# Hybrid encoder block: weight-piece rings of five places instead of four, room taken from GpSimd's DMA scratch, and a head whose ScalarE queue issues two loads

## The chip, the cores and the metric

The kernel runs on one core of a Trainium2 chip. The metric is the device time of one launch in microseconds (us); lower is better. A profile is one execution recorded by the hardware profiler. The engines are named as the profile names them: PE is the matrix engine (PEld its weight loads), DVE is VectorE, ACT is ScalarE, POOL is GpSimd, SP is SyncE. ACTq, SPq and POOLq stand for the DMA issues of these engines. TensorE's granted clock is a fraction of full speed.

## The reference

One encoder layer on a batch of 512 tokens and another of 256, 768 tokens in all, in float32. Cut to what matters:

```python
h = rmsnorm(x, ln_mix_g)
z = h @ w_in                       # 2048 -> 2560: [fourier 1024 | q 1024 | k 256 | v 256]
of = fourier_mix(zf, w_fourier)    # Re(fft2) per channel group, then a 128x128 map
oa = window_attention(rope(q), rope(k), v, attn_sink)      # 16 heads, window +-128
mixed = concat([rmsnorm(of, g_f), rmsnorm(oa, g_a)])
x = x + mixed @ w_out              # 2048 -> 2048
h = rmsnorm(x, ln_mlp_g)
u = relu(h @ w_up)                 # 2048 -> 8192
x = x + (u * u) @ w_down           # 8192 -> 2048
y = rmsnorm(x, ln_final_g)
```

## The kernel before

**Arithmetic.** Every float32 operand of a product is split in two float32r parts: a high part, which ACT makes by a rounding copy, and a low part, which DVE makes by subtracting the high part from the source. A product is then three matmuls, high by high, high by low and low by high. So each piece of a weight matrix passes four stations: a DMA on SP's queue brings a raw piece of 512 KB into the pool `wpool` (tag `raw`, two places), ACT writes the high part (`wh`, four places), DVE writes the low part (`wl`, four places), and PE uses both. A place of `wh` or `wl` is free again when the last matmul that reads it is done. A place takes 4 KB of each of SBUF's 128 partitions.

**Stages, in the order of the program.**

- Head (0 to 44 us): the v projection. `load_k` brings 16 slices `xk` of x, transposed, `split_x` scales them by the norm's gains (`gains`, a small table) and splits them into `hh` and `hl`. `load_wv` brings v's columns of w_in in four tiles `wr` of four slices each, and `split_wv` splits them. The matmuls are in `v_step` (L222, product `pv`). The tokens' norms come from rows of x (`xt`, L215). The order of the instructions on ACT, DVE and SP is the order of the code here. ACT's queue issues `gains`, the first two `wr` tiles (the first in three parts) and `ident`, before ACT's first computation. SP's queue issues the slices of x.
- Projection of q, k and the fourier group (44 to 387 us): 36 pieces of w_in through `wsplit` (L82), 48 matmuls to a piece (L542, product `pz`), with the rotation of q and k and the fourier transforms beside it.
- Attention, and the fourier half of the output projection (387 to 603 us). w_out comes in 32 pieces of two k-slices by 512 columns, numbered i = 0 to 31. `out_load(i)` issues the load, `out_high(i)` (L163) makes the high part and `out_low(i)` (L174) the low part. Pieces 0 to 15 belong to the fourier half (four blocks n of 512 output columns, four pieces to a block), pieces 16 to 31 to the attention half. The matmuls are in `proj_step` (L739, product `pm`): 24 of them, eight k-steps of three, for one row block m of 128 tokens and one n. In this stage all engines run by a planned order: `job` states each piece of work with its engine, a cost, a due time and what it has to follow, and the list scheduler `in_turn` puts the jobs of all engines in one order (by the earliest possible start and then by the due time). The jobs ("hi", i) and ("lo", i) follow `last` (L801), the last matmul of the piece i-4, which leaves the place of the ring to the piece i. The job ("load", i) follows hi and lo of the piece i-2, which leaves its raw place.
- The attention half of the output projection (603 to 751 us): block by block, n = 0 to 3, each with three groups of two row blocks; a group has eight k-steps of six matmuls. GpSimd's queue adds the fourier half onto x (`yp<-y`, L944, two transfers to a group). Pieces 20 to 31 are split here, and ACT, DVE and SP are put in order by the framework's scheduler.
- The MLP up (751 to 1685 us, `pu` L1034) and down (1685 to 2599 us, `pd` L1315), in a Strassen-like scheme of fewer products. Weight pieces go through the same two rings: `up_high` (L1013), `up_low` (L1019) and the sums of pieces (L1290).
- The tail (to 2611 us): the last residual, the final norm, and the store.

PE's own order is the order of the code in all stages. POOL's DMAs are those whose descriptors are made in software; they take their room from a scratch area in SBUF, of 16,384 bytes of each partition unless the program states another figure (L1503).

Of the kernel before, what the change touches and what calls it, by code (L numbers as in the profile page):

```python
# [11 lines left out]
F32 = mybir.dt.float32  # L12
F32R = mybir.dt.float32r
# [27 lines left out]
def hybrid_encoder(ctx: ExitStack, tc: tile.TileContext, a: dict):  # L41
# [37 lines left out]

    def wsplit(raw, g=None):  # L80

        hi = wpool.tile(raw.shape, F32R, tag="wh", name="wh", bufs=4)  # L82
        lo = wpool.tile(raw.shape, F32R, tag="wl", name="wl", bufs=4)
        if g is None:
            split(hi[:], lo[:], raw[:])
        else:
            for i in range(raw.shape[1]):
                split(hi[:, i, :], lo[:, i, :], raw[:, i, :], g(i))
        return hi, lo
# [70 lines left out]
    def out_high(i):  # L160
        half, n, j = out_seq[i]
        raw = raws[i]
        wh = wpool.tile([P, 2, 512], F32R, tag="wh", name="wh", bufs=4)  # L163
        if half:
            for r in range(2):
                nc.scalar.activation(wh[:, r], raw[:, r], AF.Copy, scale=gcat[:, 8 + 2 * j + r : 9 + 2 * j + r])
        else:
            nc.scalar.activation(wh[:], raw[:], AF.Copy)
        out_w[half, n].append((wh, None))

    def out_low(i):
        half, n, j = out_seq[i]
        raw, wh = raws.pop(i), out_w[half, n][j][0]
        wl = wpool.tile([P, 2, 512], F32R, tag="wl", name="wl", bufs=4)  # L174
        if half:
            for r in range(2):
                nc.vector.scalar_tensor_tensor(  # L177
                    out=wl[:, r], in0=raw[:, r], scalar=gcat[:, 8 + 2 * j + r : 9 + 2 * j + r], in1=f32(wh[:, r]),
                    op0=ALU.mult, op1=ALU.subtract,
                )  # L180
        else:
            nc.vector.tensor_tensor(out=wl[:], in0=raw[:], in1=f32(wh[:]), op=ALU.subtract)  # L182
        out_w[half, n][j] = (wh, wl)
# [8 lines left out]
    with ExitStack() as ph:  # L192
# [9 lines left out]
        with tc.tile_pool(name="xp", bufs=2, reuse_waits="tile") as xp:  # L202

            def load_x(m):
                xt = xp.tile([P, D], F32, tag="xt", name=f"xt{m}", bufs=2)
                nc.sync.dma_start(xt[:], x_rows(m))
                return xt

            def load_k(k):
                xk[k] = xp.tile([P, T], F32, tag="xk", name="xk", bufs=7)  # L210
                for t in (slice(0, HALF), slice(HALF, T)) if k == 0 else (slice(0, T),):
                    nc.sync.dma_start(xk[k][:, t], a["x_t"][k * P : (k + 1) * P, t])

            def row_norm(m, xt):
                nc.scalar.activation(xt[:], xt[:], AF.Square, accum_out=ss0[:, m : m + 1])  # L215
                rsqrt_of(r0[:, m : m + 1], ss0[:, m : m + 1], D, 1, nc.gpsimd)

            def v_step(k, n, ms):
                j, i = k // 4, k % 4
                l, r = ((hh, 0), (hl, 0), (hh, 1))[n]  # L220
                for m in ms:
                    nc.tensor.matmul(  # L222
                        pv[m][:, :256], l[j][:, i, m * P : (m + 1) * P], wv[j][r][:, i, :],
                        start=(k == 0 and n == 0), stop=(k == NK - 1 and n == 2),
                    )

            def v_take(m):
                pg = pv[m][:, :256].rearrange("p (g d) -> p g d", g=NKV)
                split(vhl[:, m, :, 0, :], vhl[:, m, :, 1, :], pg, r0[:, m : m + 1])

            def row_scale(m):

                dg = zp.tile([P, T], F32, tag="zs", name="dg")[:, :P]
                nc.gpsimd.tensor_scalar(
                    out=dg, in0=ident[:], scalar1=r0[:, m : m + 1], scalar2=1.0, op0=ALU.mult, op1=ALU.mult
                )
                pb = pp.tile([P, 512], F32, tag="f", name="pb", bufs=2)
                nc.tensor.matmul(pb[:, :P], ones[:], dg, start=True, stop=True)
                nc.scalar.copy(rb[:, m * P : (m + 1) * P], pb[:, :P])

            def load_wv(j, queue):
                pool, tag = (xp, "wr") if j < 2 else (wpool, "raw")
                wr = pool.tile([P, 4, 256], F32, tag=tag, name="wr", bufs=2)
                for i in ((0, 1), (1, 2), (2, 4)) if j == 0 else ((0, 4),):
                    i = slice(*i)
                    queue.dma_start(wr[:, i], w_in[:, 4 * j : 4 * j + 4, IN_W - 256 :][:, i])
                raw_v[j] = wr
                wv[j] = [wpool.tile([P, 4, 256], F32R, tag=c, name=c, bufs=4) for c in ("wh", "wl")]

            def split_wv(j, i):  # L250
                i = slice(*i)
                split(wv[j][0][:, i], wv[j][1][:, i], raw_v[j][:, i])

            def split_x(k, t=slice(0, T)):
                j, i = k // 4, k % 4
                split(hh[j][:, i, t], hl[j][:, i, t], xk[k][:, t], gains[:, k : k + 1])

            xk, xts, raw_v, wv, done = {}, {}, {}, {}, []
            pv = [pp.tile([P, 512], F32, tag="ps", name="pv") for _ in range(NM)]
            hand = ("Activation", "DVE", "SP")  # L260
            with tc.manual_schedule(engines={getattr(mybir.EngineType, e) for e in hand}):
                nc.scalar.dma_start(gains[:], a["c_gains"])
                load_wv(0, nc.scalar)
                for k in range(7):
                    load_k(k)
                    if k == 1:
                        load_wv(1, nc.scalar)
                nc.scalar.dma_start(ident[:], a["c_ident"])
                split_x(0, slice(0, HALF))
                split_wv(0, (0, 1))  # L270
                split_x(0, slice(HALF, T))
                split_wv(0, (1, 2))
                for k in range(NK):
                    if k + 1 < NK:
                        split_x(k + 1)
                    if k == 0:
                        split_wv(0, (2, 4))
                    if k % 4 == 2 and k // 4 < 3:
                        split_wv(k // 4 + 1, (0, 4))
                    if k + 7 < NK:  # L280
                        load_k(k + 7)
                    if k in (0, 3):
                        load_wv(2 + k // 3, nc.sync)
                    if k in (8, 9):
                        xts[k - 8] = load_x(k - 8)
                    for n in range(3):
                        v_step(k, n, range(NM if k < 8 else 4))
                for m in range(4):
                    row_norm(m, xts[m])
                    if m + 2 < NM:  # L290
                        xts[m + 2] = load_x(m + 2)
                for k in range(8, NK):
                    for n in range(3):
                        v_step(k, n, (4, 5))
                for m in range(NM):
                    if m >= 4:
                        row_norm(m, xts[m])
                    v_take(m)
# [499 lines left out]
    for i in range(3, 22):  # L798
        half, n, j = out_seq[i]
        need = 6 * SLOT * (n + 4 * half) + 1.4 * j  # L800
        last = ("mm", out_seq[i - 4][1], NM - 1, 2 * out_seq[i - 4][2] + 1) if i >= 4 else None  # L801
        job(("load", i), SP, 1.5, need - 14, lambda i=i: out_load(i), ("hi", i - 2), ("lo", i - 2), start=-22, wait=5)
        if i < 20:
            job(("hi", i), ACT, 1.2 if half else 0.96, need - 5, lambda i=i: out_high(i), ("load", i), last, ("<", ("hi", i - 1)), start=8.3 * i - 24)
# [205 lines left out]

    def up_high(u, s):
        raw = uw[u, steps[s][0]]
        wh = wpool.tile([P, 4, 256], F32R, tag="wh", name="wh", bufs=4)  # L1013
        nc.scalar.activation(wh[:], raw[:], AF.Copy)  # L1014
        ux[u, s] = (raw, wh)

    def up_low(u, s):
        raw, wh = ux[u, s]
        wl = wpool.tile([P, 4, 256], F32R, tag="wl", name="wl", bufs=4)  # L1019
        nc.vector.tensor_tensor(out=wl[:], in0=raw[:], in1=f32(wh[:]), op=ALU.subtract)  # L1020
        ux[u, s] = (wh, wl)

# [258 lines left out]
    def sums(u):  # L1281
# [5 lines left out]
        for t, o in ws:  # L1287
            if o is not None:
                add(t, o, ALU.subtract if i in (2, 3) else ALU.add)
            wh = wpool.tile([P, 1024], F32R, tag="wh", name="wh", bufs=4)  # L1290
            wl = wpool.tile([P, 1024], F32R, tag="wl", name="wl", bufs=4)
            nc.scalar.activation(wh[:], t[:], AF.Copy)  # L1292
            whl.append((wh, wl, t))
        if len(ss) > 1:
# [195 lines left out]
def _layouts(given):  # L1490
# [2 lines left out]
    return {  # L1493
        "x_t": np.concatenate([given["x_prompt"], given["x_sample"]], 0).T,
        "c_gains": np.concatenate(gains).reshape(3 * NK, P).T,
    }


# [23 lines left out]
```

## Time and profile before

| | us |
|---|---|
| time, median of 3 runs | 2613.86 (2612.37 to 2613.91) |
| the profiled execution's own time | 2613.02 |
| its span in the trace | 2611.2 |
| PE busy | 2584.0 (99% of the span), 13556 matmuls |
| DVE busy | 1702.9 (65%) |
| ACT busy | 1048.1 (40%) |
| POOL busy | 245.2 (9%) |
| matmuls start | 7.79 |
| last matmul ends | 2599.5 |

The span runs from the first to the last instruction; the time of the profiled execution has 1.8 us around it. PE is occupied nearly all the time, so the page's shares alone do not say what an edit around PE may be worth; the waits of PE, the stretches in which it stood still, and the two ends without any matmul do. These lines are shown in the prediction. "Busy" of a matmul overlaps with the next one's, so the distance between the starts of two matmuls (0.173 us at 384 columns, 0.227 us at 512 columns in undisturbed stretches) is the better measure of PE's pace.

### The profile page before, as it was taken

Reading aid. Unit: us, or ns where it says so; the run is one execution under the profiler, and the core shown is the slowest. Engines: PE = TensorE matmul, PEld = TensorE weight load, DVE = VectorE, ACT = ScalarE, POOL = GpSimd, SP = SyncE. Lnnn points to the kernel's source line nnn. Section 1 sums busy time; section 2 is a strip of 40 time slices with the busy share of each in tenths; the row PEclk is TensorE's granted clock in tenths of the full one; section 3 lists DMA queues with packets and bytes.
Section 4 is the critical chain, followed back from the end, with each engine's and each line's share of the span. In section 5 each row is a group of like instructions: output and inputs, shape, how many; then the busy total and the mean of one; then the engine's idle time right before and its main releaser. Section 6 shows DMA issues by size and latency. Waiting matters only on the chain.

```text
span 2611.2 us, 34913 instructions
## 1 busy us (share of the span) xinstructions
PE 2584.0 (99%) x13556; PEld 2363.5 (91%) x13556; DVE 1702.9 (65%) x2085; ACT 1048.1 (40%) x1506; POOL 245.2 (9%) x357
## 2 busy tenths in 40 slices
PE   8999999999999999999999999999999999999998
PEld 8999998887899999999999999988888888888886
DVE  4344546775655665555877787767776765777677
ACT  6233316664333333333544454433333333333335
POOL 1011212332100011000000000010000000000000
PEclk9999999999999999999999999999999999999999
DMA  8333577557774545448666666685543662554364
GB/s 298 118 116 126 161 236 208 151 140 183 216 216 153 176 164 179 173 164 317 205 211 215 231 232 210 206 338 177 181 159 111 216 235 81 178 180 160 99 210 147
DMA packets 278982, 488.23 MB, mean 187 GB/s; under 512 B 21216, under 2 KB 171488, under 8 KB 277792
## 3 DMA queue, kind: packets, MB, share of 16 engines
q1 hardware_dynamic: 202240, 329.91, 39.5%
q10 hardware_dynamic: 54576, 96.58, 9.7%
q0 software_dynamic: 22000, 59.52, 8.2%
q8 instruction: 106, 1.74, 0.3%
q14 instruction: 60, 0.49, 0.1%
HBM read 359.30 MB, written 126.62 MB: 186 GB/s over the span
## 4 chain that ended last, share of the span: by engine, by line
PE 80%; DMA 3%; DVE 2%; ACT 1%; issue 1%; POOL 0%; SPq 0%; ACTq 0%; POOLq 0%; DVEq 0%
PE pu L1034 36%; PE pd L1315 34%; PE pm L739 7%; DMA raw<-in_w_out 1%; DMA qh<-rh 1%; PE s L584 1%; PE o L655 1%; PE t L638 1%; DMA ry<-zq 0%; DMA zq<-zs 0%; PE ptx L132 0%; DVE wl L182 0%; DMA oar<-oadl 0%; DVE wl L177 0%; DVE acc L1249 0%
## 5 line engine op out<-in xcount | busy, mean ns | idle before, releaser
L1034 PE MATMUL pu<-xf,wh 128*128 128x384 f32 x3328 | 848.7, 336 | 0.0
L1034 PEld LDWEIGHTS pu<-xf,wh 128*128 128x128 f32 x3328 | 600.5, 188 | 1.7 <-ACT o L1052 1.2
L1034 PE MATMUL pu<-xf,wl 128*128 128x384 f32 x1664 | 559.1, 336 | 0.0
L1315 PE MATMUL pd<-wh,sh 128*128 128x512 f32 x1320 | 513.5, 389 | 0.0
L1315 PE MATMUL pd<-wl,sh 128*128 128x512 f32 x1320 | 513.5, 389 | 0.0
L1315 PE MATMUL pd<-wh,sl 128*128 128x512 f32 x1320 | 513.5, 389 | 0.0
L1292 ACT ACTIVATE wh<-rd 128x1024 fp32r<-128x1024 f32 x200 | 202.2, 1054 | 524.1 <-PE pd L1315 425.1
L1302 DVE TENSOR_TENSOR wl<-rd,wh 128x1024 fp32r<-128x1024 f32 x200 | 236.1, 1221 | 229.3 <-ACT wh L1292 228.7
L1014 ACT ACTIVATE wh<-ur 128x1024 fp32r<-128x1024 f32 x160 | 169.9, 1062 | 374.1 <-PE pu L1034 209.1
L1034 PEld LDWEIGHTS pu<-xf,wl 128*128 128x128 f32 x1664 | 312.8, 188 | 0.0
L1315 PEld LDWEIGHTS pd<-wh,sl 128*128 128x128 f32 x1320 | 247.8, 188 | 51.5
L1315 PEld LDWEIGHTS pd<-wl,sh 128*128 128x128 f32 x1320 | 247.8, 188 | 51.3
L1315 PEld LDWEIGHTS pd<-wh,sh 128*128 128x128 f32 x1320 | 247.8, 188 | 51.3
L1020 DVE TENSOR_TENSOR wl<-ur,wh 128x1024 fp32r<-128x1024 f32 x160 | 195.5, 1222 | 81.5 <-ACT wh L1014 78.4
L1055 DVE TENSOR_TENSOR o<-pu,o 128x768 f32<-128x768 f32 x160 | 152.9, 956 | 118.2 <-PE pu L1034 114.4
L542 PE MATMUL pz<-hh,wh 128*128 128x384 f32 x576 | 147.4, 336 | 0.0
L542 PE MATMUL pz<-hh,wl 128*128 128x384 f32 x576 | 146.4, 334 | 0.9 <-DVE wl L68 0.9
L542 PE MATMUL pz<-hl,wh 128*128 128x384 f32 x576 | 146.2, 334 | 0.0
L1285 DVE TENSOR_TENSOR rd<-rd 128x1024 f32<-128x1024 f32 x112 | 131.7, 1217 | 0.0
L1014 ACT ACTIVATE wh<-sx 128x1024 fp32r<-128x1024 f32 x64 | 67.9, 1062 | 127.7 <-PE pu L1034 99.4
L542 PEld LDWEIGHTS pz<-hh,wl 128*128 128x128 f32 x576 | 104.0, 188 | 1.3 <-DVE wl L68 1.3
L1305 DVE TENSOR_TENSOR sl<-sr,sh 128x768 fp32r<-128x768 f32 x110 | 104.6, 951 | 0.0
(210 smaller groups left out, 3463.9 us busy)
## 6 DMA issues: line engine op xcount, KB each, us to landing
rd<-in_w_down SPq DMA_DIRECT2D x176, 512.0 KB, 5.3
ur<-in_w_up SPq DMA_DIRECT2D x128, 512.0 KB, 4.0
sr<-sd SPq DMA_DIRECT2D x94, 384.0 KB, 5.5
pd<-o ACTq DMA_DIRECT2D x64, 384.0 KB, 2.3
o<-pd POOLq DMA_DIRECT2D x64, 384.0 KB, 6.2
sd<-sm ACTq DMA_DIRECT2D x60, 384.0 KB, 2.6
raw<-in_w_in SPq DMA_DIRECT2D x36, 512.0 KB, 3.6
raw<-in_w_out SPq DMA_DIRECT2D x32, 512.0 KB, 5.5
```

What stands on the lines that cost most here:

```text
L542: nc.tensor.matmul(ps[c][s][:, :HALF], w[:, i, cs], h[j][:, i, s * HALF : (s + 1) * HALF], start=first and n == 0, stop=last and n == 2,)
L584: nc.tensor.matmul(st["s", h], st["qs"][:, h, :], kd[:, g, k0 * P : k0 * P + nk], start=(n == 0), stop=(n == 1))
L739: nc.tensor.matmul(ps[:], l(k), w[:, k % 2, :], start=(k == 0 and n == 0), stop=(k == 7 and n == 2))
L1014: nc.scalar.activation(wh[:], raw[:], AF.Copy)
L1020: nc.vector.tensor_tensor(out=wl[:], in0=raw[:], in1=f32(wh[:]), op=ALU.subtract)
L1034: nc.tensor.matmul(ps[:, t, :HALF], w[:, i, t * P : (t + 1) * P], xb[:, o, i, :], start=(s == first_of[bank] and i == 0 and n == 0), stop= ...
L1055: nc.vector.tensor_tensor(out=o, in0=src, in1=o, op=ALU.add)
L1285: add = lambda x, y, op: nc.vector.tensor_tensor(out=x[:], in0=x[:], in1=y[:], op=op)
L1292: nc.scalar.activation(wh[:], t[:], AF.Copy)
L1302: nc.vector.tensor_tensor(out=wl[:], in0=t[:], in1=f32(wh[:]), op=ALU.subtract)
L1305: nc.vector.tensor_tensor(out=sl[:], in0=sr[:], in1=f32(sh[:]), op=ALU.subtract)
L1315: nc.tensor.matmul(ps[m][:, ns], l[:, q, ts], w[:, ns], start=(j == 0 and q == 0 and t == 0), stop=(j == HP // 2 - 1 and q == 1 and t == 2),)
```

## The change

**Rings.** `wh` and `wl` get five places each instead of four, at every line where one of their tiles is made. That is 8 KB more of each partition, and `dynamic_dma_scratch_size=8192` takes these 8 KB from the scratch area of POOL's DMAs. In the planned stage `last` names the piece i-5 instead of i-4.

**Head.** ACT's queue issues two loads, `gains` and the first slice of the first `wr` tile. Then a small Square of six columns of the constant tile `mhalf` is put ahead of ACT's other work (its result, in `ss0`, is overwritten later). The other slices of the first `wr` tile, the second tile and `ident` are issued on SP's queue, between the slices of x. A new input `w_v` holds v's 256 columns of w_in, laid out on the host so that the slices of one partition lie side by side: a row of a `wr` part is one stretch of 1, 3 or 4 KB, where it was one stretch of 1 KB to a slice.

```diff
@@ wsplit, out_high, out_low, up_high, up_low, the sums of pieces
-        hi = wpool.tile(raw.shape, F32R, tag="wh", name="wh", bufs=4)
-        lo = wpool.tile(raw.shape, F32R, tag="wl", name="wl", bufs=4)
+        hi = wpool.tile(raw.shape, F32R, tag="wh", name="wh", bufs=5)
+        lo = wpool.tile(raw.shape, F32R, tag="wl", name="wl", bufs=5)
...
@@ load_wv
-            def load_wv(j, queue):
-                pool, tag = (xp, "wr") if j < 2 else (wpool, "raw")
-                wr = pool.tile([P, 4, 256], F32, tag=tag, name="wr", bufs=2)
-                for i in ((0, 1), (1, 2), (2, 4)) if j == 0 else ((0, 4),):
+            def load_wv(j, queue, parts=((0, 4),)):
+                if j not in raw_v:
+                    pool, tag = (xp, "wr") if j < 2 else (wpool, "raw")
+                    raw_v[j] = pool.tile([P, 4, 256], F32, tag=tag, name="wr", bufs=2)
+                    wv[j] = [wpool.tile([P, 4, 256], F32R, tag=c, name=c, bufs=5) for c in ("wh", "wl")]
+                wr = raw_v[j]
+                for i in parts:
                     i = slice(*i)
-                    queue.dma_start(wr[:, i], w_in[:, 4 * j : 4 * j + 4, IN_W - 256 :][:, i])
-                raw_v[j] = wr
-                wv[j] = [wpool.tile([P, 4, 256], F32R, tag=c, name=c, bufs=4) for c in ("wh", "wl")]
+                    queue.dma_start(wr[:, i], a["w_v"][:, 4 * j : 4 * j + 4][:, i])
@@ the head
                 nc.scalar.dma_start(gains[:], a["c_gains"])
-                load_wv(0, nc.scalar)
-                for k in range(7):
+                load_wv(0, nc.scalar, ((0, 1),))
+                nc.scalar.activation(ss0[:], mhalf[:, :NM], AF.Square)
+                load_k(0)
+                load_wv(0, nc.sync, ((1, 4),))
+                for k in range(1, 7):
                     load_k(k)
-                    if k == 1:
-                        load_wv(1, nc.scalar)
-                nc.scalar.dma_start(ident[:], a["c_ident"])
+                    if k == 2:
+                        load_wv(1, nc.sync)
+                nc.sync.dma_start(ident[:], a["c_ident"])
@@ the planned stage
-        last = ("mm", out_seq[i - 4][1], NM - 1, 2 * out_seq[i - 4][2] + 1) if i >= 4 else None
+        last = ("mm", out_seq[i - 5][1], NM - 1, 2 * out_seq[i - 5][2] + 1) if i >= 5 else None
@@ the host's layouts, and the program
+        "w_v": given["w_in"][:, IN_W - 256 :].reshape(NK, P, 256).transpose(1, 0, 2),
...
-    nc = bacc.Bacc("TRN2", target_bir_lowering=False, num_devices=1)
+    nc = bacc.Bacc("TRN2", target_bir_lowering=False, num_devices=1, dynamic_dma_scratch_size=8192)
```

Line numbers of the changed kernel are three or four higher from the head on. The change moves instructions at three places that matter below.

In the head, ACT's first instructions before (`wr` is v's weight tile; the numbers behind names tell tiles apart):

```order
L262 DMA gains_264<-in_c_gains 128x48
L246 DMA wr_307<-in_w_in 128x256 x2
L246 DMA wr_307<-in_w_in 128x2x256
L246 DMA wr_318<-in_w_in 128x4x256
L268 DMA ident_65<-in_c_ident 128x128
L70 ACT_TABLE_LOAD
L70 ACTIVATE hh0_286<-xk_313,gains_264 128x384
L67 ACTIVATE wh_311<-wr_307 128x256
```

and ACT's first instructions after the change:

```order
L263 DMA gains_264<-in_c_gains 128x48
L249 DMA wr_307<-in_w_v 128x256
L265 ACT_TABLE_LOAD
L265 ACTIVATE ss0_265<-mhalf_68 128x6
L70 ACTIVATE hh0_286<-xk_312,gains_264 128x384
L67 ACTIVATE wh_308<-wr_307 128x256
```

Four DMA issues have left ACT, and the load of its function table stands ahead of the first instruction that needs data from a DMA.

At the end of the projection of q, ACT's rows around the high part of the last piece of w_in (`wh_3830`) before; `rh` is the high part of a rotated q, `qh2` and `ql2` are where q's parts are stored:

```order
L70 ACTIVATE rh_3822<-rx_3812 128x384
L458 DMA qh2_88<-rh_3822 128x384
L459 DMA ql2_89<-rl_3823 128x384
L67 ACTIVATE wh_3830<-raw_3828 128x1024
L70 ACTIVATE rh_3906<-rx_3896 128x384
```

and after:

```order
L70 ACTIVATE rh_3664<-rx_3654 128x384
L462 DMA qh2_88<-rh_3664 128x384
L463 DMA ql2_89<-rl_3665 128x384
L67 ACTIVATE wh_3830<-raw_3828 128x1024
L70 ACTIVATE rh_3743<-rx_3733 128x384
L462 DMA qh2_88<-rh_3743 128x384
L463 DMA ql2_89<-rl_3744 128x384
L70 ACTIVATE rh_3822<-rx_3812 128x384
```

The high part of that piece has moved ahead of the splits of two queries (`rh_3743` and `rh_3822`).

At the boundary between the two halves of the output projection, ACT's rows before; the two rows with `gains` ahead of `xc` are the pieces 16 and 17, the two behind it 18 and 19 (a piece is two instructions); `xc` takes the last result of the fourier half, `oar` and `oah5` belong to the norm of the attention rows:

```order
L705 ACTIVATE oar_6304<-oar_6304 128x512
L166 ACTIVATE wh_6431<-raw_6058,gains_264 128x512 x2
L166 ACTIVATE wh_6439<-raw_6081,gains_264 128x512 x2
L752 ACTIVATE xc_6466<-pm_6415,r1_267 128x512
L166 ACTIVATE wh_6469<-raw_6459,gains_264 128x512 x2
L166 ACTIVATE wh_6475<-raw_6464,gains_264 128x512 x2
L696 ACTIVATE oah5_6478<-oar_6409 128x512
```

and after, where the first two are the pieces 17 and 18:

```order
L709 ACTIVATE oar_6312<-oar_6312 128x512
L166 ACTIVATE wh_6439<-raw_6076,gains_264 128x512 x2
L166 ACTIVATE wh_6447<-raw_6126,gains_264 128x512 x2
L756 ACTIVATE xc_6474<-pm_6423,r1_267 128x512
L166 ACTIVATE wh_6477<-raw_6467,gains_264 128x512 x2
L700 ACTIVATE oah5_6483<-oar_6417 128x512
L700 ACTIVATE oah5_6483<-oar_6419 128x512
L166 ACTIVATE wh_6764<-raw_6472,gains_264 128x512
```

The piece 16 has left this place. Its two instructions now stand five row blocks earlier on ACT, ahead of the `xc` of the last column block's first row block (`es` and `ob` belong to the attention):

```order
L618 ACTIVATE es_6057<-es_6057 128x4
L166 ACTIVATE wh_6083<-raw_5991,gains_264 128x512 x2
L666 COPY ob_6104<-o_6072 128x512
L756 ACTIVATE xc_6120<-pm_6019,r1_267 128x512
```

In the same way the first piece of each other column block behind the first (the pieces 4, 8 and 12) stands four or five row blocks earlier on ACT than before, and the load of the piece two behind it as much earlier on SP's queue. Of the four pieces of a block, ACT then has two at the place where it had the first two, now the second and the third, and one where it had the last two.

More of the change, by code (lines that the diff above doesn't have):

```diff
@@ L162, in out_high @@
         raw = raws[i]
-        wh = wpool.tile([P, 2, 512], F32R, tag="wh", name="wh", bufs=4)
+        wh = wpool.tile([P, 2, 512], F32R, tag="wh", name="wh", bufs=5)
         if half:
@@ L173, in out_low @@
         raw, wh = raws.pop(i), out_w[half, n][j][0]
-        wl = wpool.tile([P, 2, 512], F32R, tag="wl", name="wl", bufs=4)
+        wl = wpool.tile([P, 2, 512], F32R, tag="wl", name="wl", bufs=5)
         if half:
@@ L1012, in up_high @@
         raw = uw[u, steps[s][0]]
-        wh = wpool.tile([P, 4, 256], F32R, tag="wh", name="wh", bufs=4)
+        wh = wpool.tile([P, 4, 256], F32R, tag="wh", name="wh", bufs=5)
         nc.scalar.activation(wh[:], raw[:], AF.Copy)
@@ L1018, in up_low @@
         raw, wh = ux[u, s]
-        wl = wpool.tile([P, 4, 256], F32R, tag="wl", name="wl", bufs=4)
+        wl = wpool.tile([P, 4, 256], F32R, tag="wl", name="wl", bufs=5)
         nc.vector.tensor_tensor(out=wl[:], in0=raw[:], in1=f32(wh[:]), op=ALU.subtract)
@@ L1289, in sums @@
                 add(t, o, ALU.subtract if i in (2, 3) else ALU.add)
-            wh = wpool.tile([P, 1024], F32R, tag="wh", name="wh", bufs=4)
-            wl = wpool.tile([P, 1024], F32R, tag="wl", name="wl", bufs=4)
+            wh = wpool.tile([P, 1024], F32R, tag="wh", name="wh", bufs=5)
+            wl = wpool.tile([P, 1024], F32R, tag="wl", name="wl", bufs=5)
             nc.scalar.activation(wh[:], t[:], AF.Copy)
```

## The prediction

> **What bounds the kernel now.** I read the waits of PE first, since PE is busy nearly all the span. The columns are: who waited for what, us in total, times, the longest.
>
> ```profile
> PE pv L222 <- ACT wh L67: 7.8, 1, 7.8
> PE pm L739 <- ACT wh L166: 2.3, 1, 2.3
> PE pm L739 <- DVE wl L182: 2.1, 4, 0.8
> PE pm L739 <- DVE wl L177: 1.4, 3, 0.7
> PE pz L542 <- DVE wl L68: 0.9, 1, 0.9
> ```
>
> The first row is the head: no matmul starts before 7.79 us. The four others, 6.7 us in nine waits, are parts of weight pieces that came late. To see what each costs I read the stretches around them and the timeline. First the stretches (start and end; length; busy time of PE, PEld, DVE, ACT, POOL; granted clock; DMA share; GB/s):
>
> ```profile
> 608.00:616.00 8.00, 5.43 (x16) 3.81 (x15) 4.44 (x7) 4.87 (x8) 1.76 (x2) 0.79 0.76 252
> ...
> 654.00:2599.50 1945.50, 1945.46 (x9883) 1770.54 (x9881) 1343.48 (x1302) 757.71 (x874) 104.92 (x179) 1.00 0.57 191
> ```
>
> From 654 us to its last matmul PE never stands still. More places can bring nothing there: the MLP's 1945 us, three quarters of the span, stay. The kernel is PE's work, plus the head, plus the nine waits, plus the tail. Then the timeline of PE at one wait:
>
> ```profile
> 650.49 0.39 PE L739 MATMUL pm<-wh,oah 128*128 128x512 f32 x1
> 651.54 0.50 PE L739 MATMUL pm<-wl,oah 128*128 128x512 f32 x1 [0.67 <-DVE wl L177]
> 651.88 0.39 PE L739 MATMUL pm<-wh,oal 128*128 128x512 f32 x1
> ```
>
> Undisturbed, these matmuls start 0.227 us apart (the spacing given with the profile). Here it is 1.05, so the stop takes 0.82: the wait shown and 0.16 more, because a matmul's recorded 0.39 overlaps with the next. The step behind it is 0.34, another 0.11. So I count each wait **plus 0.27 us**.
>
> **The change part by part: the rings.** By that count, stop by stop. The sums go against the profiled execution: 2613.02 us, its span of 2611.2 and 1.8 around it, 0.8 under the median of 2613.86.
>
> *378 us.* The last piece of w_in:
>
> ```profile
> 376.90 1.06 ACT L67 ACTIVATE wh<-raw 128x1024 fp32r<-128x1024 f32 x1 [1.60 <-DVE rl L71]
> ...
> 378.02 0.61 PE L542 MATMUL pz<-hh,wh 128*128 128x384 f32 x2
> ...
> 379.92 0.62 PE L542 MATMUL pz<-hh,wl 128*128 128x384 f32 x2 [0.94 <-DVE wl L68]
> ```
>
> ACT stood idle 1.60 us behind DVE's `rl`, a rotated query that has nothing to do with the piece; the high part came behind it in the order, the low part behind that. Cost: 0.94 + 0.27, and 0.25 for the high part: it was ready at 377.96, and PE's pair of matmuls at 378.02 stands that much later than its spacing of 0.173 asks (the list of waits leaves it out). Together 1.46. With five places ACT's row moves ahead of two queries' splits (order above). It then hangs on its place, which is free a piece earlier (48 matmuls of 0.173, 8.3 us). **Removed: 1.46.**
>
> *393 us.* Piece 3 of w_out, a wait of 0.55, so 0.82:
>
> ```profile
> 391.51 1.06 ACT L168 ACTIVATE wh<-raw 128x1024 fp32r<-128x1024 f32 x1 [9.65 <-DMA raw<-in_w_out]
> ```
>
> ACT waited for a transfer, not for a place. Its raw place and SP's order around it are unchanged. **Stays.**
>
> *448 us.* A wait of 0.77, so 1.04. SP's two loads and PE:
>
> ```profile
> 435.90 3.93 SPq L77 DMA_DIRECT2D raw<-in_w_out  x2
> ...
> 449.16 0.50 PE L739 MATMUL pm<-wl,ofh 128*128 128x512 f32 x1 [0.77 <-DVE wl L182]
> ```
>
> The two issues are the pieces 6 and 7; the second, 3.5 us behind the first, waits for the low part of piece 5 and lands just before ACT converts it. After the change piece 4 is made four row blocks earlier, 5 has 4's place in the order, and the load of 7 has that of 6: 3.5 us earlier, against a stop of 1.0. **Removed: 1.04.**
>
> *562 to 567 us.* The same pattern with the pieces 14 and 15, two waits, 0.75 + 0.54:
>
> ```profile
> 563.97 0.50 PE L739 MATMUL pm<-wl,ofh 128*128 128x512 f32 x1 [0.41 <-DVE wl L182]
> ...
> 566.44 0.50 PE L739 MATMUL pm<-wl,ofh 128*128 128x512 f32 x1 [0.34 <-DVE wl L182]
> ```
>
> Here ACT and DVE did four pieces in a row beside the attention; piece 12 now goes ahead, and each later one moves up by one. **Removed: 1.29.**
>
> *608 us,* the largest. ACT's and SP's rows, then PE's:
>
> ```profile
> 600.20 2.55 ACT L166 ACTIVATE wh<-raw,gains 128x512 fp32r<-128x512 f32 x4
> ...
> 603.49 1.70 SPq L77 DMA_DIRECT2D raw<-in_w_out  x2
> ...
> 610.10 2.60 ACT L166 ACTIVATE wh<-raw,gains 128x512 fp32r<-128x512 f32 x4 [6.21 <-DMA raw<-in_w_out]
> ```
>
> ```profile
> 610.88 0.49 PE L739 MATMUL pm<-wh,oah 128*128 128x512 f32 x1 [2.27 <-ACT wh L166]
> 611.67 0.59 PE L739 MATMUL pm<-wl,oah 128*128 128x512 f32 x1 [0.29 <-DVE wl L177]
> 612.06 0.63 PE L739 MATMUL pm<-wh,oal 128*128 128x512 f32 x1
> ...
> 615.42 0.39 PE L739 MATMUL pm<-wl,oah 128*128 128x512 f32 x1
> ```
>
> Pieces 16 and 17 are converted at 600, when places come free. Only then can 18 and 19 be loaded (603.49), 6.6 us before ACT has one. The first stop is 2.27 + 0.16 = 2.43, the second 0.29 + 0.27 = 0.56 with its first slow step. From 612.06 to 615.42 eight steps take 3.36 instead of 1.82: 1.5 more, at half pace, where the stretch has a granted clock of 0.79, beside 1.00 over the MLP. Together 4.5. After the change 16 is converted five row blocks earlier, so 18 is loaded long before, and 17 and 18 are converted at 600. Piece 19 is loaded when 17 has left its raw place, at 603.5 as now. The half starts at 603.0 and needs 19 three pieces later, each 12 matmuls of 0.227: 603.0 + 8.2 = 611.2. If it lands like the first of the two now, its high part is there at 610.75, its low part at 611.45. What is left is 0.1 to 0.4; I take 0.4. **Removed: 4.1.**
>
> By the Trainium skill ("TensorE: Matmul & The Clock Gate", Part 1), the clock halves after an idle window of about 3.4 us, on a window that runs freely. The gap here, 2.43 us, is shorter, so a strict reading would leave the 1.5 us in place and give a sum 1.5 higher; the trace shows the slow steps just behind the gap and at no other stop, so the sum does not follow it.
>
> *650 us.* Two waits, 0.67 and 0.41, with 0.54: 1.62. DVE's low part of piece 22 stands half ahead of, half behind a row that waits for POOL. Now it is piece 23 that stands there, two k-steps (2.7 us) later in PE's order; 22 goes ahead with 21. **Removed: 1.62.**
>
> Rings: 1.46 + 1.04 + 1.29 + 4.1 + 1.62 = **9.5**. In bounds: the 378 and 608 stops alone (5.6) if the new order brings as much lateness elsewhere, up to all nine stops (10.8).
>
> **The head.** ACT and PE:
>
> ```profile
> 1.18 1.94 ACTq L246 DMA_DIRECT2D wr<-in_w_in  x4
> 5.08 0.35 ACTq L268 DMA_DIRECT2D ident<-in_c_ident  x1
> 5.52 1.28 ACT L70 ACT_TABLE_LOAD   x1 [5.52 <-DMA wr<-in_w_in]
> 6.82 0.61 ACT L70 ACTIVATE hh<-xk,gains 128x384 fp32r<-128x384 f32 x1
> 7.34 0.40 ACT L67 ACTIVATE wh<-wr 128x256 fp32r<-128x256 f32 x1
> 7.79 1.65 PE L222 MATMUL pv<-wh,hh 128*128 128x256 f32 x6 [7.79 <-ACT wh L67]
> ```
>
> ACT's issues hold it until 5.4; then come the table, the first high part of x, the first of v's weights, and PE. Two issues instead of six (at about half a us each, as the four above) end near 1.7, the table is loaded by 3.0, in the shadow of the first transfers. What is late next is data; the loads issued first (KB each, us to landing):
>
> ```profile
> xk<-in_x_t SPq DMA_DIRECT2D x1, 192.0 KB, 2.4
> ...
> wr<-in_w_in ACTq DMA_DIRECT2D x1, 128.0 KB, 3.9
> ```
>
> x's first half, issued at 0.73, is there at 3.1, the first weight slice, issued near 1.2, at 5.1. Its high part (0.40) and a hop give PE 5.5; alone on its queue it may land some tenths earlier, so I take 5.35, which is 2.4 earlier. The loads that left ACT now stand between x's slices on SP's queue, whose nine issues take some 8 us already.
>
> Does the gain reach the end of the head? There the rows of x decide:
>
> ```profile
> 39.00 1.92 ACT L215 ACTIVATE xt<-xt 128x2048 f32<-128x2048 f32 x1 [1.91 <-DMA xt<-in_x_prompt]
> ...
> 41.40 1.66 DVE L71 SCALAR_TENSOR_TENSOR vhl<-pv,r,vhl 128x256 fp32r<-128x256 f32 x4 [6.47 <-ACT vhl L70]
> ...
> 43.92 0.51 PE L542 MATMUL pz<-hh,wh 128*128 128x384 f32 x2
> ```
>
> The accumulators that the next stage takes over are free when the first two of these four are read, near 42.2, and its first matmul starts at 43.92: 1.7 us of slack. The rows of x come at the end of a queue that the transfers fill:
>
> ```profile
> 3.00:6.00 3.00, 0.00 (x0) 0.00 (x0) 0.00 (x0) 0.48 (x1) 0.00 (x0) 1.00 0.95 301
> ...
> 9.00:12.00 3.00, 3.00 (x19) 3.00 (x18) 2.84 (x4) 2.76 (x5) 0.00 (x0) 1.00 1.05 412
> ```
>
> At 19 matmuls in 3 us PE takes 2.8 us for the 18 matmuls of a slice, which brings 384 + 128 KB: 180 GB/s, under half of what the queues carry, so the slices keep ahead of it in the new order too. The rows of x, behind them, can end earlier only by what they do better before 6 us: at 400 instead of 301 GB/s that is 0.7 us of the three. With 0.5 of it the end may move by 2.2, less than PE's 2.4. **Head: 2.2**; bounds 1.0 (0.8 lost to later transfers, or a first slice no earlier than 5.8) and 2.9 (a slice landed at 4.5 and the whole 0.7).
>
> **GpSimd's room.** The trace shows its transfers but not their room:
>
> ```profile
> q0 software_dynamic: 22000, 59.52, 8.2%
> yp<-y POOLq DMA_DIRECT2D x24, 256.0 KB, 5.8
> ```
>
> 8.2% of the DMA engines' span is a nearly empty queue; I take 0. The other end is the third rival.
>
> **Sum:** 2613.0 - 9.5 - 2.2 = 2601.3; set on the median of before it would be 2602.1. I say **2601.5**.
>
> **The rivals.** *1. Transfers bind, not places.* Raw places stay two, and at 393 and 608 a landing was the last thing. If the pieces at 448, 562 and 650 are still late by their transfers and their neighbours in the order, 1.04 + 1.29 + 1.62 = 4.0 stays: 2605.3. For it speaks ACT's 6.21 of waiting at 610; against it that at 378 and 562 the transfer was long in and ACT or DVE were late. *2. The head's gain is given back* at 42 us, because x's rows come later by the loads now on SP's queue: 2603.5. *3. Slower: POOL's transfers queue for room.* If half the room holds no second transfer of 256 KB, the pair of `yp<-y` goes one behind the other: 2 x 5.8 + 0.9 for an issue is 12.5 us, against 48 matmuls of 0.227 to a group, 10.9. Twelve groups late by 1.6 are 19 us, and the sum 2620. It decides from the point where a single transfer takes over 4 KB of each partition's room. Against it: its landing of 5.8 is like that of plain loads, and the kernel keeps several such transfers in flight only in this stage. The Trainium skill ("Debugging Trainium Hangs", section Descriptor Overflow) speaks against the change too: too many descriptors for a carve-out of 16 KiB a partition hang the Pool queue; no run here shows how full it is. *4. New stops in the new order.* The moved pieces put 1.06 of ACT and 1.23 of DVE ahead of an attention row each; with four to six stops of 0.8 to 1.3 in place of the old ones the ring gives 3 to 5 and with a lost head 2609 to 2611. *5. The clock's slow steps stay* by the skill's rule above: 2603.
>
> **How the numbers follow.** Forecast 0.60 (own range 2599.5 to 2603.5), rival 1 0.15, rival 2 0.10, rival 5 0.03, rival 4 0.07, rival 3 0.05. The measurement can tell about 0.2%, 5.2 us, so from 2608.6 down it is faster: 0.60 + 0.15 + 0.10 + 0.03 = 0.88; same 0.07; slower 0.05. The range takes in the forecast with the bounds of its terms (9.5 to 10.8 with 2.9 gives 2599; with more of the loads hidden 2598) and the rivals 1, 2 and 5 with a shortfall beside them: 2598 to 2607.
>
> **What would show it.** Right: the first `pv` near 5.4 and the first `pz` near 41.7; no waits of PE at 376, 446, 560 and 650, one of under 0.3 near 609, no slow stretch there, and 0.8 still at 391; from then on the same work 11.7 earlier. Wrong: a first `pv` above 6.5, a wait for `vhl` at 42, L177 or L182 in more than three waits, or `yp<-y` landing over 8 us.

## The result, and the profile after

| | before | after |
|---|---|---|
| time, median of 5 runs each on one chip, us | 2612.37 (2610.01 to 2613.91) | 2601.12 (2599.61 to 2601.33) |
| ratio | | 0.9954 (95% interval 0.9942 to 0.9965) |
| the profiled execution's own time / its span | 2613.02 / 2611.2 | 2601.33 / 2599.6 |
| first matmul / last matmul starts | 7.79 / 2599.07 | 5.08 / 2587.98 |

The change is 11 us faster, 0.46% by the ratio, and 2601.12 lies 0.4 us beside the 2601.5 of the prediction. How PE waits now (who waited for what, us in total, times, longest):

```profile
PE pv L222 <- ACT wh L67: 5.1, 1, 5.1
PE t L642 <- POOL p L634: 0.8, 2, 0.6
PE pm L743 <- DVE wl L182: 0.3, 1, 0.3
```

Of the nine waits for weight pieces one is left, at 390 us. The second row is new in this size: the attention's transposes wait for POOL's normalised rows. Two stretches, with the columns as in the prediction:

```profile
603.00:613.00 10.00, 10.00 (x48) 8.31 (x47) 5.77 (x10) 4.66 (x8) 1.76 (x2) 1.00 0.80 246
...
650.00:2588.00 1938.00, 1938.00 (x9853) 1765.66 (x9851) 1341.93 (x1293) 765.54 (x869) 104.97 (x179) 1.00 0.57 191
```

The first covers the end of the first pieces of the attention half, where before PE stood for 2.4 us and went at half pace after it: nothing of it is left, neither the stop nor a lowered clock.

The start of the head, ACT's rows after:

```profile
1.66 1.28 ACT L265 ACT_TABLE_LOAD   x1 [1.66 <-PEq L1508]
...
4.61 0.42 ACT L67 ACTIVATE wh<-wr 128x256 fp32r<-128x256 f32 x1 [0.48 <-DMA wr<-in_w_v]
...
7.13 0.42 ACT L67 ACTIVATE wh<-wr 128x256 fp32r<-128x256 f32 x1 [1.60 <-DMA wr<-in_w_v]
8.24 0.93 ACT L70 ACTIVATE hh<-xk,gains 128x768 fp32r<-128x768 f32 x1 [0.69 <-DMA xk<-in_x_t]
```

The table is loaded in the shadow of the first transfers, as forecast, and the first weight slice decides PE's start. Then ACT waits for the second slice of the weights and of x; before, it found both already there.

To see where the time came from I set the two traces side by side by the number of the matmul: the start of the n-th matmul before, less that of the n-th after, is PE's **lead** at this point. (The order of matmuls within the attention differs by a few, so single values there are good to some tenths.)

| before's time of it, us | lead, us | the step, us | forecast of the step |
|---|---|---|---|
| 8 (the second matmul) | 2.70 | | 2.4 |
| 20 | 1.86 | -0.84 | |
| 44, first `pz` | 1.86 | head together 1.86 | 2.2 |
| 388 | 3.28 | +1.42 (at 378: 1.47) | 1.46 |
| 420 | 2.03 | -1.25 (at 395 it was 3.48) | 0 |
| 447 | 2.11 | +0.08 | |
| 451 | 3.34 | +1.23 | 1.04 |
| 561 | 2.38 | -0.96 | 0 |
| 568 | 3.67 | +1.29 | 1.29 |
| 603 | 3.47 | -0.20 | 0 |
| 617 | 8.20 | +4.73 | 4.1 |
| 655 | 9.88 | +1.68 | 1.62 |
| 752, start of the MLP | 9.89 | 0 | 0 |
| 1300 | 11.10 | +1.21 | 0 |
| 2599, the last | 11.10 | 0 | 0 |

The spans differ by 11.6; the last 0.5 lies in the tail behind the last matmul. Every stop that the prediction removed went, at its place and nearly with its size. Three rows were not in it: 2.2 us lost in the attention, 1.2 gained in the MLP, and 0.84 lost in the first 20 us.

### The profile page after: what moved, and what is told of

The parts are those of the page before. It is cut to its first block, busy times and chain, and to the rows that moved or that the text cites. A ratio compares the mean times of both kernels' runs of the same rounds, so it can differ in the third digit from the quotient of the medians.

```text
span 2599.6 us, 34859 instructions
## 1 busy us (share of the span) xinstructions
PE 2580.8 (99%) x13556; PEld 2363.6 (91%) x13556; DVE 1703.4 (66%) x2085; ACT 1057.3 (41%) x1507; POOL 248.5 (10%) x357
## 4 chain that ended last, share of the span: by engine, by line
PE 97%; DVE 1%; DMA 1%; POOL 1%; ACT 1%; issue 0%; SPq 0%; POOLq 0%; ACTq 0%; DVEq 0%
PE pu L1038 36%; PE pd L1319 35%; PE pz L546 12%; PE pm L743 9%; PE pv L222 1%; PE t L642 1%; PE o L659 1%; PE s L588 1%; PE pa L363 1%; POOL p L634 1%; PE pe L384 0%; PE ptx L132 0%; DMA ry<-zq 0%; DMA zq<-zs 0%; PE pc L331 0%
## 5 line engine op out<-in xcount | busy, mean ns | idle before, releaser
L1296 ACT ACTIVATE wh<-rd 128x1024 fp32r<-128x1024 f32 x200 | 211.9, 1060 | 515.3 <-PE pd L1319 261.4
L1306 DVE TENSOR_TENSOR wl<-rd,wh 128x1024 fp32r<-128x1024 f32 x200 | 243.0, 1223 | 221.4 <-ACT wh L1296 216.5
L546 PEld LDWEIGHTS pz<-hl,wh 128*128 128x128 f32 x576 | 104.1, 188 | 0.0
```

The costliest lines, as they stand in the source:

```text
L546: nc.tensor.matmul(ps[c][s][:, :HALF], w[:, i, cs], h[j][:, i, s * HALF : (s + 1) * HALF], start=first and n == 0, stop=last and n == 2,)
L1306: nc.vector.tensor_tensor(out=wl[:], in0=t[:], in1=f32(wh[:]), op=ALU.subtract)
```

## The experiments

Medians stand beside the kernel before on the same chip.

**The head alone.** From the changed kernel:

```diff
-        wh = wpool.tile([P, 2, 512], F32R, tag="wh", name="wh", bufs=5)
+        wh = wpool.tile([P, 2, 512], F32R, tag="wh", name="wh", bufs=4)      # and at the eight other places
-        last = ("mm", out_seq[i - 5][1], ...
+        last = ("mm", out_seq[i - 4][1], ...
-    nc = bacc.Bacc("TRN2", target_bir_lowering=False, num_devices=1, dynamic_dma_scratch_size=8192)
+    nc = bacc.Bacc("TRN2", target_bir_lowering=False, num_devices=1)
```

> The head of the change alone: rings of four, the full scratch, the plan as before. Theory (the two parts add up): the first pv near 5.1, the first pz 1.8 to 1.9 earlier than in the kernel before, all nine waits of PE for weight pieces still there, and the time 1.9 us under the kernel before. Rival (the transfers between 388 and 403 us stand still whatever PE does, so the queries' rows come no earlier): PE's lead falls below 1 us by 420 us and the time is under 1 us lower. What is open besides: whether the lead of 1.9 is smaller than what the transfers allow.

Measured: 2612.51 against 2613.29, ratio 0.9993 (0.9984 to 1.0003). The interval takes in no change at all as well as a gain of 1.9, so the runs neither show nor refute it. The trace does better: the first `pv` at 5.32, seven of the nine waits for pieces (those at 393 and 653 have fallen below what the list shows), the lead 2.15 at 20 us, 1.29 at 44 us, 1.20 at 388 us, 1.43 at 420 us. So nothing is lost between 388 and 420, and the rival's "under 1" is not met. But 0.86 goes at the end of the head, where a row of the timeline names what the prediction had as the head's limit:

```profile
42.42 0.83 PE L546 MATMUL pz<-hh,wh 128*128 128x384 f32 x2 [0.48 <-DVE vhl L71]
```

The next stage's first matmul waits until DVE has read the accumulators, and that hangs on the rows of x.

**The rings alone.** From the kernel before:

```diff
-        hi = wpool.tile(raw.shape, F32R, tag="wh", name="wh", bufs=4)
+        hi = wpool.tile(raw.shape, F32R, tag="wh", name="wh", bufs=5)      # and at the eight other places
-        last = ("mm", out_seq[i - 4][1], ...
+        last = ("mm", out_seq[i - 5][1], ...
+    nc = bacc.Bacc("TRN2", ..., dynamic_dma_scratch_size=8192)
```

> The rings alone: five places, the plan with i-5, half the scratch, the head as before. Theory (parts add up): the head's 7.8 us as before, the wait at 378 gone, and the time 9 to 10 us under the kernel before. Theory A (the 1.2 us that the changed kernel loses near 403 us come from transfers that let PE gain only about 2 us there): with a lead of only 1.5 us from 378 nothing is lost at 403. Theory B (they come from the moved piece 4, whose high and low part stand ahead of an attention unit's rows): the 1.2 us are lost here too, and the lead at 420 us is under 0.5.

Measured: 2602.79 against 2613.29, ratio 0.9956 (0.9942 to 0.9971), or 10.5 us. The rings are nearly the whole change: its median lies 1.7 over the changed kernel's 2601.12, and the intervals of the two ratios overlap. The lead is -0.50 at 44 us (the old head, started 0.2 earlier, lost more on the way), 1.15 at 388, 0.66 at 395 (PE waits 0.8 for piece 3), 0.49 at 406 and 0.94 at 420. Nothing like 1.2 is lost around 403, though piece 4 is moved here too: Theory B does not hold.

**The old plan with five places.** From the changed kernel:

```diff
-        last = ("mm", out_seq[i - 5][1], ... if i >= 5 else None
+        last = ("mm", out_seq[i - 4][1], ... if i >= 4 else None
```

> The changed kernel, but the planned stage follows the piece i-4 again, as if the ring had four places; the places, the head and the scratch are as changed. The stops at 448 (1.1), 562 (1.3) and 608 (4.7) should come back, the one at 378 not: 7 us over the changed kernel if Theory A holds (the loss near 403 stays), 6 us if Theory B holds (the loss goes, since piece 4 is back at its place). If the places alone and not the order were what counts, it would be within 1 us of the changed kernel.

Measured: 2608.74, ratio 0.9984 (0.9974 to 0.9993), 7.6 over the changed kernel's 2601.12, which was measured at another time. The waits for weight pieces at 448, 562 and 608 are back, the one at 378 and those at 650 are not (the lead gains 1.47 and 1.68 there), nor are the MLP's. Of this profile's last lead of 3.28 the head has 1.35, so the places without the order keep, on balance, 1.9 of the 9.2 that the changed kernel gains behind its head, about a fifth; that they alone count is refuted. The lead of 3.00 at 388 falls to 0.92 at 395 and 0.85 at 403 with piece 4 at its old place. What takes it here is not `p`: PE waits 1.3 and 0.8 for the parts of piece 3, and the granted clock is half from 393.5 to 396.9 us (the last section has the rows). The loss stays, as under Theory A, but another transfer takes it.

**A quarter of GpSimd's scratch,** in the kernel before:

```diff
-    nc = bacc.Bacc("TRN2", target_bir_lowering=False, num_devices=1)
+    nc = bacc.Bacc("TRN2", target_bir_lowering=False, num_devices=1, dynamic_dma_scratch_size=4096)
```

> The kernel before with a quarter of GpSimd's DMA scratch (4096 bytes a partition), nothing else. Theory (the room is never short): time and the landings of yp<-y, o<-pd and oar<-oadl as before, within 0.2%. Rival (the room binds): a pair of yp<-y one behind the other, landings over 8 us, and 10 us or more on the time; then half the scratch may already cost a little.

Measured: 2612.78 against 2613.29, ratio 0.9995 (0.9986 to 1.0005). The landings of the transfers of `yp<-y` (least, median, most) in this kernel, then in the kernel before:

```profile
DMA to landing us min/median/max: 3.9/5.2/8.8
```

```profile
DMA to landing us min/median/max: 3.9/5.8/8.8
```

At a quarter of the room the time does not move and `yp<-y` is no slower; of the others that were named, `o<-pd` lands in 6.3 instead of 6.2 us in the median and `oar<-oadl` in 6.7 instead of 6.1. So half of the room costs nothing that these runs can tell.

**The head's loads in another order:**

```diff
-                load_wv(0, nc.sync, ((1, 4),))
+                load_wv(0, nc.sync, ((1, 2),))
                 for k in range(1, 7):
                     load_k(k)
+                    if k == 1:
+                        load_wv(0, nc.sync, ((2, 4),))
```

> The changed kernel, but on SP's queue only the second slice of the first wr tile goes ahead of x's second slice, the third and fourth behind it. Theory (what the changed head gives back between 5 and 20 us, 0.85 of its 2.7, is the wait for x's second slice behind 384 KB of weights): PE's first k-steps stand closer, and PE's lead over the kernel before at 20 us is 2.3 to 2.6 instead of 1.86. Rival (the rows of x decide at 42 us): the lead at 20 us grows, but a wait for vhl appears and the lead at 44 us is again 1.9 or less. Second rival (the second k-step then waits for its third weight slice): nothing gained at 20 us.

Measured: 2601.5, ratio 0.9959 (0.9944 to 0.9974): as the changed kernel. The lead at 20 us is 1.42, not 2.3 to 2.6, and at 44 us 0.41, with 0.6 of waiting for `vhl`. My theory of the first 20 us fell. Which transfer holds PE there stays open.

**The queries' rows first.** From the changed kernel, two start times of the plan:

```diff
-        job(("of", m), SP, 3.0, SLOT * m - 20, ..., start=-22 if m < 2 else SLOT * m - 20, wait=4)
+        job(("of", m), SP, 3.0, SLOT * m - 20, ..., start=-22 if m < 2 else 8.5 if m == 2 else SLOT * m - 20, wait=4)
-        job(("load", i), ..., ("hi", i - 2), ("lo", i - 2), start=-22, wait=5)
+        job(("load", i), ..., ("hi", i - 2), ("lo", i - 2), start=9.5 if i == 5 else -22, wait=5)
```

> The changed kernel, but in the plan the loads of the third row block of ofh and ofl and of piece 5 come behind the loads of the fourth group's queries. Theory A (the changed kernel loses 1.2 us near 403 because those queries' rows share the queues with 1.5 MB issued ahead of them): the rows land 2 to 4 us earlier, the wait of the transposes for POOL's p near 403 falls from 0.8 to under 0.3, and PE's lead over the kernel before is 3.0 to 3.5 at 420 us instead of 2.0; about 1 us on the time. Rival (the delayed ofh and ofl of the third row block come late): a new wait of pm near 404, nothing gained.

DVE at the rotation of the fourth group's queries, in the kernel before, in the changed one, and (below) with three raw places:

```profile
401.65 0.68 DVE L488 TENSOR_TENSOR ry<-ry,sinr 64x512 f32<-64x512 f32 x1 [0.49 <-DMA ry<-zq]
```

```profile
400.32 0.68 DVE L492 TENSOR_TENSOR ry<-ry,sinr 64x512 f32<-64x512 f32 x1 [2.51 <-DMA ry<-zq]
```

PE came to this point 3.3 us earlier, the rows only 1.3 us. DVE takes its instructions in order, and behind the rotation stand the row sums that POOL needs for `p`, and `p` is what PE's transposes wait for:

```profile
404.25 1.22 PE L642 MATMUL t<-ident,p 128*128 128x128 f32 x6 [0.60 <-POOL p L634]
```

The transfers themselves (KB each, us from issue to landing), in the changed kernel and with the queries' rows first:

```profile
rx<-zq SPq DMA_DIRECT2D x1, 128.0 KB, 7.0
ry<-zq SPq DMA_DIRECT2D x2, 64.0 KB, 6.6
```

```profile
rx<-zq SPq DMA_DIRECT2D x1, 128.0 KB, 2.8
ry<-zq SPq DMA_DIRECT2D x2, 64.0 KB, 2.7
```

Issued within half a us of the same time, but ahead of 1.5 MB instead of behind it, they land 4 us sooner, DVE no longer waits, and the wait for `p` near 403 is gone. The lead goes from 2.54 at 388 to 2.59 at 420: nothing is lost on balance, but the 3.0 to 3.5 of Theory A are not reached. The profile had a late head (0.89 at 44 us), and the changed kernel's own second profile, below, has no wait near 403 either with 2.67 at 388. So this run shows what the order does to the landing, and not yet that it saves PE the wait. The time is 2600.68, ratio 0.9958 (0.9941 to 0.9974): no gain by the medians.

**Three raw places.** From the changed kernel:

```diff
-    def wload(src, na, nb, pool=wpool, bufs=2):
+    def wload(src, na, nb, pool=wpool, bufs=3):      # and the other tiles of this tag
-        job(("load", i), ..., ("hi", i - 2), ("lo", i - 2), start=-22, wait=5)
+        job(("load", i), ..., ("hi", i - 3), ("lo", i - 3), start=-22, wait=5)
-    nc = bacc.Bacc(..., dynamic_dma_scratch_size=8192)
+    nc = bacc.Bacc(..., dynamic_dma_scratch_size=4096)
```

> The changed kernel with three raw places instead of two for the same pieces, the room taken from the scratch again (4096 bytes left), and the plan's loads follow the piece i-3. Theory (raw places bind nowhere any more): PE's lead by stage as in the changed kernel within 0.5 us, the time within 1 us of it. Rival (loads were late for want of a raw place): the wait at 390 us (0.3) goes, and the time is 0.5 to 1.5 lower; or the earlier loads crowd the queues near 390 us and the queries' rows come later still, 1 us slower.

Measured: 2604.54, ratio 0.997 (0.9961 to 0.9979), 3 us slower than the two runs above on the same chip (2601.5 and 2600.68), whose times all lie below its own. The wait at 390 is gone as the rival said (the lead rises to 3.66 at 395), and then:

```profile
402.08 0.68 DVE L492 TENSOR_TENSOR ry<-ry,sinr 64x512 f32<-64x512 f32 x1 [4.61 <-DMA ry<-zq]
```

```profile
PE t L642 <- POOL p L634: 4.6, 4, 2.4
```

The lead falls to 1.40 at 406 and to -2.32 at 420. Pieces that come sooner crowd out the rows that are needed first. Some 2 of this loss is not the wait itself: the granted clock is 0.50 from 405.3 to 412.1 us, and nine steps in it take 0.427 us instead of 0.227.

**Queries and piece 3 first,** and the changed kernel again on the same chip:

```diff
-        ... start=-22 if m < 2 else 8.5 if m == 2 else SLOT * m - 20, wait=4)
+        ... start=(-22, -6.0, 8.5)[m] if m < 3 else SLOT * m - 20, wait=4)
```

> The kernel of the run with the queries' rows first, and besides the loads of the second row block of ofh and ofl behind those of the pieces 3 and 4. Theory (the 0.9 us that PE still loses at 390 is piece 3 landing behind 2 MB of ofh and ofl): piece 3 lands 2 to 3 us earlier, the wait for its low part (0.7) goes, PE's lead over the kernel before is 0.5 to 1.0 larger at 420 us than with the queries' rows alone for the same lead at 388, and the time is 1 to 2 us under the changed kernel's of the same chip. Rival (the second row block then comes late): a wait near 395, nothing gained; or the queries' rows come later again and the wait near 403 comes back.

> The changed kernel, unaltered, beside the run above on one chip: 2600 to 2602 us, and a second profile of it. If the lead of the head is settled by the transfers of the moment, its lead at 44 us will not be 1.86 again but anywhere between 0.9 and 1.9; if it is settled by the program, it will be 1.8 to 1.9. The wait near 403 (0.8 in two) should be there when the lead at 388 is above 3, and smaller when it is under 2.5.

Measured: 2598.81 (2598.20 to 2603.01) for the new order, 2601.31 (2601.15 to 2604.88) for the changed kernel beside it, 2612.39 for the kernel before; ratios 0.9951 (0.9939 to 0.9964) and 0.9962 (0.9949 to 0.9976). The intervals overlap, so by times alone the order of the two is likely but not settled; the traces show where PE comes earlier. The waits of PE in the new order:

```profile
PE pv L222 <- ACT wh L67: 5.5, 1, 5.5
PE t L642 <- POOL p L634: 0.2, 1, 0.2
```

Not one piece is waited for; piece 3 lands at 385.3 us, in the changed kernel's two profiles at 387.9 and 389.6. The stretch of the old wait at 390, in the changed kernel beside it and in the new order:

```profile
384.00:392.00 8.00, 6.93 (x34) 5.37 (x32) 3.65 (x10) 1.06 (x1) 0.00 (x0) 1.00 1.00 383
```

```profile
384.00:392.00 8.00, 7.99 (x40) 6.77 (x40) 4.72 (x16) 3.48 (x11) 0.32 (x1) 1.00 0.80 309
```

The lead grows from 2.96 at 388 to 4.96 at 403 and 5.08 at 420, where the changed kernel's falls from 2.67 to 2.11, and ends at 13.8 instead of 11.1. With a lead at 403 larger than in any other run, the wait for `p` near 403 does not come: this is what the run with the queries' rows first had left open. The 2.1 that it grows is more than the 0.5 to 1.0 expected: by the starts of its matmuls the kernel before loses 0.82 at 393, three times 0.34 between its transposes at 398 and 0.18 at 405, together 2.0, and the new order has no such step between 386 and 427. That the crowding already cost the kernel before these 2.0 fits, since the later loads of ofh and ofl are all that the new order adds to the run with the queries' rows first, which keeps three steps of 0.46 near 396.

The changed kernel's second profile has a lead of 1.15 at 44 us where the first had 1.86, 2.67 at 388, and 0.2 of waiting for `p`. So the program alone does not settle the lead of the head; that the transfers of the moment do is the likely reason, and no run isolates it. The other half stays open: 2.67 lies between the two bounds that I had set. And a lead above 3 is not needed for the loss: with the old kernel's order and a quarter of the scratch DVE waited 2.42 for the same rows at 402 us, PE 1.1 for `p`, and the lead fell from 1.59 at 403 to -1.95 at 420, half-clock steps included. This second profile of the changed kernel pays at 390 instead, 0.8 and 0.4 for piece 3, and comes out with the same 2.1 at 420.

## Why the prediction was right, point by point

- **The rings, 9.5.** The removed stops gave 1.47, 1.23, 1.29, 4.73 and 1.68, together 10.4 against 9.5 forecast. Reading the stops off the starts of matmuls, each wait plus 0.27, was right to a tenth at 378, 562 and 650; at 448 it gave 1.04 for 1.23. The stop at 393 that was to stay, 0.82, cost 0.58 in this profile and 1.7 in the changed kernel's second one.
- **608, 4.1 and measured 4.73.** The sum of 4.5 had left out one slow step, the 0.39 ahead of 612.06, which is 0.16 over the usual spacing. And the 0.4 set aside for a rest was not needed: piece 19, loaded at 599.24 just after piece 17 had left its place, was being converted at 605.56, and PE reached it at 599.5 + 8.2 = 607.7.
- **The MLP, 0 and measured 1.2.** The step that failed is "From 654 us to its last matmul PE never stands still. More places can bring nothing there". It rested on PE's busy time, which overlapping matmuls fill even where they are stretched. The waits of PE's weight loads showed it; before and after:

```profile
PEld pu L1034 <- ACT o L1052: 1.2, 6, 0.3
```

```profile
PEld pu L1038 <- ACT o L1056: 0.2, 1, 0.2
```

  PE's weight load waits there for ACT to take a finished product. With four places the row reads 1.1 to 1.2 (before, the head alone, a quarter of the scratch), with five it is 0 to 0.2 (0.6 in the last order), and the lead gains nothing from 752 to 1300 with four, 0.8 to 1.3 with five. The old plan with five places differs from the head alone in nothing but the places and the scratch, and gains 1.1 here: so the places bring it. How they free ACT was not tested.
- **The attention, 0 and measured -2.2.** The prediction had "transfers bind, not places" as a rival for the stops at 448, 562 and 650, with 4.0. There it was wrong. The transfers bind at 388 to 403, where PE, coming earlier, meets rows that come only a part of that earlier: 1.25 in this profile. The rest, 0.96 from 451 to 561, is the rival of new stops in a small form: the transposes' weight loads wait for `p` more often there. Before (451 to 562 us) and after (448 to 560 us, the same work):

```profile
PEld t L638 <- POOL p L630: 0.3, 1, 0.3
```

```profile
PEld t L642 <- POOL p L634: 1.3, 5, 0.3
```

  The five other profiles with i-5 and two raw places lose 0.8 to 0.9 there with four or five such waits, at the same two places (504 and 558 us in this profile), whether their lead is 2 or 6; no profile under the old plan has more than one. So these waits come with the new order. Two profiles under the old plan lose as much, but by another wait, for `tl` near 529 (the old plan with five places 1.1, the quarter of the scratch 0.8). Which moved piece makes `p` late is not shown.
- **The head, 2.2 and measured 1.86** in this profile, with a first `pv` at 5.08 instead of 5.35. Seven profiles with this head have a lead of 0.9 to 1.9 at 44 us, 1.3 in the mean; the three with the old head 0, -0.5 and -1.4. The difference of the means is 1.9. The limit at the end of the head, by `vhl`, shows as a wait of PE or its weight loads in three of the seven. But the time alone does not show the head (0.9993, 0.9984 to 1.0003).
- **GpSimd's room, 0**: right, even at a quarter.

That the total came out within half a us is partly luck, since errors cancel: 2.2 lost in the attention and 0.3 in the head, against 1.2 in the MLP, 0.9 at the stops and 0.5 in the tail.

## What to carry to other kernels

A stall's price is the distance of two matmuls' starts less their usual spacing; PE's busy time hides a part of each stall, and the waits of PE's weight loads show it. What a deeper ring is worth is decided by the order that it allows: the places alone gave, on balance, a fifth here, and earlier loads without an eye to what else shares the queue cost 3 us. When many stops go at once, ask which transfers did not move with the engine: their landing is the next bound, and putting the small, urgent ones ahead of the large ones gave the lowest median of all, 2598.81, though its interval overlaps with the changed kernel's.

## What the runs showed of the hardware

PE's half pace behind a stop is not settled by the stop's length. In the kernel before, 2.66 us from start to start at 608 and 0.79 for the next step were followed by nine steps of 0.38 to 0.43 instead of 0.227. In the head alone 2.36 and 0.79 were followed by one of 0.59 and such steps until 612.8; in the run with the old plan 2.20 and 0.79 were followed by three quicker steps and then by eight of 0.42 to 0.43 until 615.35. In the run with a quarter of the scratch 2.38 and 0.79 were followed by none: the next steps are 0.34 and then 0.23. The granted clock of the 4 us behind the stop, in the kernel before and in that run:

```profile
611.00:615.00 4.00, 3.71 (x9) 2.68 (x10) 3.80 (x6) 3.51 (x7) 1.76 (x2) 0.62 0.58 181
```

```profile
615.00:619.00 4.00, 3.65 (x15) 2.81 (x16) 3.94 (x6) 3.53 (x7) 1.65 (x2) 1.00 0.66 241
```

A stop of some 2.2 us can so cost about 1.5 us more, or not. Shorter stops lowered the clock too. In the old plan 1.66 and 1.26 us from start to start, for piece 3 at 390, were enough; with a quarter of the scratch no step between 403 and 407 was over 0.93, but PE was busy for 2.08 of 3.40 us, in part with transposes. The stretch ahead and the one at half clock, first in the old plan, then with a quarter of the scratch:

```profile
390.10:393.50 3.40, 1.37 (x6) 0.93 (x6) 1.94 (x6) 1.46 (x3) 0.00 (x0) 1.00 0.76 300
393.50:396.90 3.40, 3.40 (x13) 2.94 (x12) 0.64 (x3) 2.21 (x10) 1.17 (x3) 0.50 0.84 251
```

```profile
403.10:406.50 3.40, 2.08 (x13) 1.31 (x12) 2.61 (x10) 1.68 (x3) 2.57 (x4) 1.00 0.21 47
406.55:409.95 3.40, 3.40 (x11) 2.85 (x11) 2.58 (x11) 1.60 (x4) 0.00 (x0) 0.50 0.90 187
```

Each stretch at half clock before the tail lasted 3.4 us, but 6.8 with three raw places, and the two of the old plan begin at 393.49 and 611.94, 218.45 us or 64 times 3.413 apart. This fits the freely running window of 3413 ns of the Trainium skill ("TensorE: Matmul & The Clock Gate", Part 1), but not its condition of a whole idle window: PE was partly busy in the window ahead each time.
